# Mixed rows written to DRAM already transposed, block by block, by the vector engine

## The chip, the cores and the metric

The kernel runs on one core of one Trainium2 chip. The metric is the device time of one execution in microseconds (us). The engines named below are TensorE (PE; PEld is its weight load), VectorE (DVE), ScalarE (ACT), GpSimd (POOL) and SyncE (SP, which here only issues DMAs).

## The reference

Two layers of a token mixer over 2048 latent tokens and 256 context tokens, width 1024, in fp32. Cut to what matters here:

```python
h = layer_norm(x) * (1 + scale) + shift                  # and hc from the context
parts = split_cols(h @ w_in)                             # 15 groups of columns
hg  = bidirectional_recurrence(hgrn2_inputs(...))        # 256 wide, chunks of 64 tokens
gla = bidirectional_recurrence(gla_inputs(...))          # 256 wide
mla = softmax_attend(q, concat(k_c, k), concat(v_c, v))  # 4 heads, 512 wide, 2304 keys
y = concatenate([gated_head_norm(hg), mla * silu(mgate), gated_head_norm(gla)], -1)
x_new = layer_norm(ALPHA * x + gate * (y @ w_out)) * ln_g + ln_b
```

The last layer computes `x_new` for the latent tokens alone.

## The kernel before, in words

Tokens go in tiles of 128 (18 tiles, the first two are context) and in pairs of tiles (9 pairs). Each layer has three stages, and every intermediate goes through DRAM scratch (`scratch`, L111).

- `project` (L270): layer norm and the product with `w_in`, each fp32 operand split into a high and a low part, with three matmuls for a product.
- `mix` (L974): attention and the two recurrences, interleaved. Per tile, `attend` (L885) does two rounds of two heads: scores `pss`, exponentials `sx`, transposes of them `ptp`, split into `ph` (ACT) and `pl` (DVE), products `oc`, then `poa`, which DVE scales and gates into `ym` (L969). Per pair, `recur` (L668) works through six levels, POOL scaling keys `ka` and queries `qa` with decay products `t`; the level-0 product lies in a buffer of tag `t0` (L723). `chunk_outputs` (L796) takes the pair's output `o` (ACT, L821, into the one buffer of tag `acc`), squares it into a `t0` buffer (`sq`), reduces that on DVE (`rss`, L826 and L827), takes the power on POOL (`rrs`, L90) and multiplies twice on POOL (L830, L831).
- Both write rows of `y` (tokens by features) to DRAM: `recur` columns 0 to 511 of a pair at L832, `attend` columns 512 to 1023 of a tile at L972.
- `output` (L1040): per tile, `turned` (L1070) loads 128 rows of `y`, turns them with 8 TensorE transposes into `pty`, and splits them into `yhl` (ACT high, DVE low). 48 matmuls (two halves of 512 columns, 8 blocks of features, 3 products) go into `pzo`, and DVE forms `z` from them. `turned(t + 1)` stands ahead of the matmuls of tile t.

All engines run their instructions in order. The order on each engine is set when the kernel is built: a scheduler follows a simulated timeline, with priorities (`AHEAD`, `SOON`, `EARLY`). DMAs issued from SP go round eight completion counters (`DMAHW0` to `DMAHW7` in the order listings), and a DMA waits for the earlier one on its counter. Buffers of later stages lie on those of earlier ones, so the first writes of `output` wait for the last readers in `mix`.

Of the kernel before, what the change touches and what calls it, by code (L numbers as in the profile page):

```python
# [7 lines left out]
F32 = mybir.dt.float32  # L8
# [3 lines left out]
ALU = mybir.AluOpType  # L12
# [4 lines left out]
P = 128  # L17
D = 1024
KD = D // P
# [35 lines left out]
class Trunk:  # L55
# [55 lines left out]
    def scratch(self, l):  # L111

        d, c, nt = self.dpool, self.cpool, self.nt
        S = {}
# [11 lines left out]
        S["sb"] = d.tile([P, self.npairs, NCH, 3, 64], F32, name=f"dsb{l}")  # L126
        S["y"] = d.tile([nt, D], F32, name=f"dy{l}")
        return S
# [501 lines left out]
    def pair_rows(self, nat, p, c0, c1):  # L630
        return nat[p * SEG:(p + 1) * SEG, c0:c1].rearrange("(j p) n -> p j n", p=P)

    def back_states(self, S, rp, rps):

        nc = self.nc
# [4 lines left out]
        for p in list(range(ncp))[::-1] + list(range(ncp, self.npairs))[::-1]:  # L640
            f = rp.tile([P, 1 + L3], F32, tag="fa", name="bf")
            nc.gpsimd.memset(f[:, 0:1], 0.0)
            nc.sync.dma_start(out=f[:, 1:].rearrange("p (b n) -> p b n", b=3), in_=S["F"][:, p, 0])
            k = rp.tile([P, 3, SEG], F32, tag="ka", name="bk")
# [151 lines left out]
    def chunk_outputs(self, S, rp, rps, p, acc, qa, qm, v2, vt, sbt, sts):  # L796
        nc = self.nc
        po = rps.tile([P, 2, 512], F32, tag="R", name="po")
        quads = ((0, 0), (1, 1), (1, 0), (0, 1))
        for j in range(2):  # L800
            for sl in range(4):
                for e, c in quads:
                    rows = slice(64 * e, 64 * e + 64)
                    o = 256 * j + 64 * sl
# [26 lines left out]
        nc.gpsimd.tensor_tensor(o, o, vt[:, :, 512:1024], op=ALU.mult)  # L831
        nc.sync.dma_start(out=self.pair_rows(S["y"], p, 0, 512), in_=o)  # L832

# [51 lines left out]
    def attend(self, S, K, ap, aps, G, t, j):  # L885
        nc = self.nc
# [4 lines left out]
        nc.sync.dma_start(out=mg, in_=S["nat"][t * P:(t + 1) * P, 1024:1536])  # L891
        ym = ap.tile([P, 512], F32, tag="ym", name="ym")
        for hp in range(2):
# [70 lines left out]
            for i in range(2):  # L964
                nc.tensor.matmul(po[:, i, :], os_[:, i * P:(i + 1) * P], S["uv"][:, 2 * hp + i, :],  # L965
                                 start=True, stop=True)
            for i in range(2):
                hs = slice((2 * hp + i) * P, (2 * hp + i + 1) * P)
                nc.vector.scalar_tensor_tensor(out=ym[:, hs], in0=po[:, i, :], scalar=rinv[i], in1=mg[:, hs],  # L969
                                               op0=ALU.mult, op1=ALU.mult)  # L970
            yield
        nc.sync.dma_start(out=S["y"][t * P:(t + 1) * P, 512:1024], in_=ym)  # L972

    def mix(self, l, S):  # L974

        nc = self.nc
        with ExitStack() as ctx:
            rp = self.pool(ctx)
            ap = Route(lambda: self.pool(ctx), "os mx nm sm ri", "mg", "ym", "ph pl", "cth ctl ks", "cq cqh cql",
                       "qn ropt ropa ropb", "rh rl", "qh ql", "cnh cnl", "sx")  # L980
# [59 lines left out]
    def output(self, l, S):  # L1040
        nc, io = self.nc, self.io
        last = l == DEPTH - 1
        with ExitStack() as ctx:
            R = Route(lambda: self.pool(ctx), "yt", "woa", "sto mvo veo rso", "gate", "lng lnb", "z", "xto", "wob", "yhl")
            ps = Route(lambda: self.pool(ctx, psum=True), "low", "pz", "tr")
            nc.vector.memset(ps.tile([P, 512], F32, name="low")[:, 0:1], 0.0)
# [23 lines left out]
            def turned(t):  # L1070
                yt = R.tile([P, D], F32, tag="yt", bufs=2, name="yt")
                nc.sync.dma_start(out=yt, in_=S["y"][t * P:(t + 1) * P, :])
                yhl = R.tile([P, 2, KD, P], F32R, tag="yhl", bufs=2, name="yhl")
                yh, yl = yhl[:, 0], yhl[:, 1]
                for q in range(2):
                    pt = ps.tile([P, 4, P], F32, tag="tr", bufs=2, name="pty")
                    for i in range(4):
                        k = 4 * q + i
                        nc.tensor.transpose(pt[:, i, :], yt[:, k * P:(k + 1) * P], self.ident)  # L1079
                    self.split(yh[:, 4 * q:4 * q + 4, :], yl[:, 4 * q:4 * q + 4, :], pt)  # L1080
                return yh, yl
# [142 lines left out]
```

## Time and profile before

| | |
|---|---|
| median of 3 runs | 3767.64 us (3766.39 to 3768.89) |
| the profiled execution: its time | 3762.88 us |
| the profiled execution: its span | 3761.1 us |
| mean granted TensorE clock | 0.99 of full speed |
| PE busy | 3621.1 us (96%) |
| DVE busy | 2139.0 us (57%) |
| ACT busy | 1435.7 us (38%) |
| POOL busy | 812.2 us (22%) |
| DMA, queue of SP | 403 MB, 33.7% of 16 engines |

Busy time is the union of an engine's instructions over the span of the profiled execution. Matmuls overlap: a group's mean duration is longer than what one of them adds to the busy time. Layer 0's `mix` runs from about 640 to 1740 us, its `output` to about 1960; layer 1's `mix` from about 2580 to 3570, its `output` to the end.

### The profile page before, as it was taken

The page shows a single profiled execution, that of the slowest core. Times are in us where ns is not written, and L with a number is a line of the kernel's source. Part 1 is how long each engine was busy: PE and PEld are TensorE (multiplying, and loading weights), DVE is VectorE, ACT ScalarE, POOL GpSimd, SP SyncE. Part 2 cuts the span into 40 slices and gives each one's busy share as a digit, 9 for nine tenths or more (in the row PEclk, how much of TensorE's full clock was granted, in tenths as well). Part 3 has the DMA queues.
Part 4 walks back from the last instruction along what each step waited for, and adds up shares of the span by engine and source line. Part 5 has one row for each costly group of instructions (what it writes and reads, how often), then busy time and mean ns, then how long its engine had stood idle before and what let it go on. Part 6 is the DMA issues. An engine that isn't in the chain of part 4 may idle for free. (4 is left out here: it accounts for less than half of the span.)

```text
span 3761.1 us, 84541 instructions
## 1 busy us (share of the span) xinstructions
PE 3621.1 (96%) x36056; PEld 3274.7 (87%) x36056; DVE 2139.0 (57%) x5026; ACT 1435.7 (38%) x2296; POOL 812.2 (22%) x614
## 2 busy tenths in 40 slices
PE   8999999999999999998999999999999999999999
PEld 5999999888788888887879999998888888888787
DVE  6764242566666666556765442425765566656566
ACT  3525242344444444442115242523443444444400
POOL 1000000001335444351110000000022344644211
PEclk9999999999999999998999999999999999999999
DMA  7774344322122112115435443433221222221342
GB/s 255 232 202 147 124 135 140 111 80 91 53 65 84 61 56 70 54 58 196 156 106 163 146 147 120 153 109 110 85 88 43 60 68 61 71 80 44 102 143 101
DMA packets 263687, 410.79 MB, mean 109 GB/s; under 512 B 39632, under 2 KB 179984, under 8 KB 262288
## 3 DMA queue, kind: packets, MB, share of 16 engines
q1 hardware_dynamic: 261872, 403.04, 33.7%
q8 instruction: 283, 4.64, 0.5%
q10 hardware_dynamic: 1440, 2.36, 0.2%
q14 instruction: 92, 0.75, 0.1%
HBM read 288.66 MB, written 116.67 MB: 108 GB/s over the span
## 5 line engine op out<-in xcount | busy, mean ns | idle before, releaser
L420 PE MATMUL pj<-wh,hl 128*128 128x256 f32 (+1 forms) x2224 | 623.8, 281 | 8.0 <-DVE hl L85 8.0
L420 PE MATMUL pj<-wh,hh 128*128 128x256 f32 (+1 forms) x2224 | 625.2, 281 | 2.0 <-DVE ve L372 1.2
L420 PE MATMUL pj<-wl,hh 128*128 128x256 f32 (+1 forms) x2224 | 624.3, 281 | 0.0
L910 DVE TENSOR_SCALAR_CACHE_REDUCE sx<-pss 128x512 f32<-128x512 f32 (+1 forms) x648 | 402.9, 632 | 204.8 <-PE pss L908 178.7
L85 DVE TENSOR_TENSOR pl<-ptp,ph 128x512 fp32r<-128x512 f32 x580 | 389.1, 686 | 183.8 <-ACT ph L79 180.6
L79 ACT CAST ph<-ptp 128x512 fp32r<-128x512 f32 x580 | 327.9, 586 | 361.8 <-PE ptp L946 349.3
L420 PEld LDWEIGHTS pj<-wh,hl 128*128 128x128 f32 x2224 | 421.1, 190 | 8.9 <-DVE hl L85 8.9
L420 PEld LDWEIGHTS pj<-wh,hh 128*128 128x128 f32 x2224 | 423.2, 190 | 2.7 <-DVE ve L372 1.6
L420 PEld LDWEIGHTS pj<-wl,hh 128*128 128x128 f32 x2224 | 421.5, 190 | 0.0
L946 PE MATMUL ptp<-ident,sx 128*128 128x128 f32 x2320 | 372.0, 278 | 25.6 <-DVE pl L85 15.7
L933 PE MATMUL oc<-ph,cnh 128*128 128x256 f32 x1160 | 340.1, 315 | 23.4 <-ACT ph L79 22.9
L920 ACT ACTIVATE sx<-sx,nm 128x2304 f32<-128x2304 f32 (+1 forms) x136 | 288.4, 2121 | 183.0 <-DVE nm L916 182.6
L431 PE MATMUL pj<-hh,wh 128*128 128x256 f32 x1136 | 321.1, 283 | 0.0
L431 PE MATMUL pj<-hh,wl 128*128 128x256 f32 x1136 | 319.9, 282 | 0.0
L431 PE MATMUL pj<-hl,wh 128*128 128x256 f32 x1136 | 319.0, 281 | 0.0
L946 PEld LDWEIGHTS ptp<-ident,sx 128*128 128x128 f32 x2320 | 273.8, 142 | 50.5 <-DVE pl L85 19.8
L85 DVE TENSOR_TENSOR wl<-wraw,wh 128x1024 fp32r<-128x1024 f32 (+1 forms) x144 | 169.4, 1211 | 238.1 <-ACT wh L79 238.0
L933 PE MATMUL oc<-ph,cnl 128*128 128x256 f32 x1160 | 303.9, 284 | 0.0
L904 PE MATMUL pss<-cth,qh 128*128 128x512 f32 (+1 forms) x648 | 264.5, 408 | 13.3 <-DVE sx L910 13.3
L933 PEld LDWEIGHTS oc<-ph,cnh 128*128 128x128 f32 x1160 | 222.1, 191 | 52.1 <-ACT ph L79 39.0
L938 PE MATMUL oc<-pl,cnh 128*128 128x256 f32 x1160 | 245.2, 294 | 0.0
L905 PE MATMUL pss<-ctl,qh 128*128 128x512 f32 (+1 forms) x648 | 242.5, 374 | 0.0
(251 smaller groups left out, 7878.0 us busy)
## 6 DMA issues: line engine op xcount, KB each, us to landing
wraw<-in_w_in_dram SPq DMA_DIRECT2D x132, 512.0 KB, 4.6
dnat<-stg SPq DMA_DIRECT2D x104, 256.0 KB, 2.1
vg<-dnat SPq DMA_DIRECT2D x17, 1024.0 KB, 6.2
yt<-dy SPq DMA_DIRECT2D x34, 512.0 KB, 3.7
wmt<-in_w_modT_dram SPq DMA_DIRECT2D x64, 256.0 KB, 3.8
fa<-dF SPq DMA_DIRECT2D x18, 768.0 KB, 4.3
ka<-dK SPq DMA_DIRECT2D x18, 768.0 KB, 4.2
dK<-stg SPq DMA_DIRECT2D x36, 256.0 KB, 4.1
```

What stands on the lines that cost most here:

```text
L79: nc.scalar.copy(hi, src)
L85: nc.vector.tensor_tensor(lo, src, hi, op=ALU.subtract)
L420: nc.tensor.matmul(pj[:, j, :n], h[pr][a][:, k, tk], w[b][:, k, :n], start=(k == 0 and a + b == 0), stop=(k == KD - 1 and a == 1))
L431: nc.tensor.matmul(pj[:, j, :], w[b][:, k, cs], h[pr][a][:, k, :], start=(k == 0 and a + b == 0), stop=(k == KD - 1 and b == 1))
L904: nc.tensor.matmul(pss[:, :n], G["qh"][hp][:, i, tk], K["cth"][:, ks], start=True, stop=False)
L905: nc.tensor.matmul(pss[:, :n], G["qh"][hp][:, i, tk], K["ctl"][:, ks], start=False, stop=False)
L910: nc.vector.tensor_scalar(sx[:, ks], pss[:, :n], SCALE, None, op0=ALU.mult, op1=ALU.max, accum_out=mx[:, nb:nb + 1])
L920: nc.scalar.activation(sx[:, :nk], sx[:, :nk], AF.Exp, bias=nm, accum_out=sm)
L933: nc.tensor.matmul(oc, K[k][:, keys(kc, c)], ph[:, c, :], start=(kc + c == 0 and k == "cnh"), stop=False)
L938: nc.tensor.matmul(oc, K["cnh"][:, keys(kc, c)], pl[:, c, :], start=False, stop=(kc + c == nch - 1))
L946: nc.tensor.transpose(pt[:, c, i, :], pexp[i][:, (kc + c) * P:(kc + c + 1) * P], self.ident)
```

## The change

The scratch tensor `y` (tokens by features) becomes `yT` (features by tokens). Before the rows are stored, DVE transposes every block of 32 by 32 elements inside a tile; the move of whole blocks is left to the DMA, in `put_turned`: one DMA for each 32 partitions, which writes pieces of 32 tokens (128 bytes) to one feature each. The recurrences write `o` through a new tile `ot` (tag `t0`) in two calls of `put_turned` (8 DMAs of 512 pieces), the attention writes each round of two heads through `yo` (4 DMAs of 256 pieces). `turned` loads a tile of `yT` with one DMA of 512-byte rows and splits it without TensorE and without PSUM.

```diff
-        S["y"] = d.tile([nt, D], F32, name=f"dy{l}")
+        S["yT"] = d.tile([D, nt], F32, name=f"dy{l}")
...
+    def put_turned(self, S, src, f0, n, t0):
+
+        for a in range(4):
+            dst = S["yT"][f0:f0 + n, t0 + 32 * a:t0 + 32 * a + 32].rearrange("(b f) t -> f b t", f=32)
+            self.nc.sync.dma_start(out=dst, in_=src[32 * a:32 * a + 32].rearrange("f (b t) -> f b t", t=32))
...
         nc.gpsimd.tensor_tensor(o, o, vt[:, :, 512:1024], op=ALU.mult)
-        nc.sync.dma_start(out=self.pair_rows(S["y"], p, 0, 512), in_=o)
+        ot = rp.tile([P, 1024], F32, tag="t0", name="ot")
+        nc.vector.transpose(out=ot, in_=of)
+        for j in range(2):
+            self.put_turned(S, ot[:, 512 * j:512 * j + 512], 0, 512, (2 * p + j) * P)
...
-        ym = ap.tile([P, 512], F32, tag="ym", name="ym")
         for hp in range(2):
...
+            ym = ap.tile([P, 256], F32, tag="ym", name="ym")
             for i in range(2):
                 hs = slice((2 * hp + i) * P, (2 * hp + i + 1) * P)
-                nc.vector.scalar_tensor_tensor(out=ym[:, hs], in0=po[:, i, :], scalar=rinv[i], in1=mg[:, hs],
-                                               op0=ALU.mult, op1=ALU.mult)
+                nc.vector.scalar_tensor_tensor(out=ym[:, i * P:(i + 1) * P], in0=po[:, i, :], scalar=rinv[i],
+                                               in1=mg[:, hs], op0=ALU.mult, op1=ALU.mult)
+            yo = ap.tile([P, 256], F32, tag="yo", name="yo")
+            nc.vector.transpose(out=yo, in_=ym)
+            self.put_turned(S, yo, 512 + 256 * hp, 256, t * P)
             yield
-        nc.sync.dma_start(out=S["y"][t * P:(t + 1) * P, 512:1024], in_=ym)
...
-            ap = Route(lambda: self.pool(ctx), "os mx nm sm ri", "mg", "ym", "ph pl", "cth ctl ks", "cq cqh cql",
+            ap = Route(lambda: self.pool(ctx), "os mx nm sm ri", "mg", "ym yo", "ph pl", "cth ctl ks", "cq cqh cql",
...
-            ps = Route(lambda: self.pool(ctx, psum=True), "low", "pz", "tr")
+            ps = Route(lambda: self.pool(ctx, psum=True), "low", "pz")
...
-                yt = R.tile([P, D], F32, tag="yt", bufs=2, name="yt")
-                nc.sync.dma_start(out=yt, in_=S["y"][t * P:(t + 1) * P, :])
+                yt = R.tile([P, KD, P], F32, tag="yt", bufs=2, name="yt")
+                nc.sync.dma_start(out=yt, in_=S["yT"].rearrange("(k p) t -> p k t", p=P)[:, :, t * P:(t + 1) * P])
                 yhl = R.tile([P, 2, KD, P], F32R, tag="yhl", bufs=2, name="yhl")
                 yh, yl = yhl[:, 0], yhl[:, 1]
                 for q in range(2):
-                    pt = ps.tile([P, 4, P], F32, tag="tr", bufs=2, name="pty")
-                    for i in range(4):
-                        k = 4 * q + i
-                        nc.tensor.transpose(pt[:, i, :], yt[:, k * P:(k + 1) * P], self.ident)
-                    self.split(yh[:, 4 * q:4 * q + 4, :], yl[:, 4 * q:4 * q + 4, :], pt)
+                    ks = slice(4 * q, 4 * q + 4)
+                    self.split(yh[:, ks, :], yl[:, ks, :], yt[:, ks, :])
```

POOL at the turn from one pair of the recurrence to the next (layer 0, the fourth such turn), before. `rrs` and the two products into `o` belong to the old pair, the others to the new one; a number behind `t` only tells buffers apart.

```order
L764 TENSOR_TENSOR ka<-ka,fa 128x384
L724 TENSOR_TENSOR t_15606<-fa 128x768 [waits DVE_49]
L90 TENSOR_TENSOR rrs<-rss,mhalf 128x16 [waits DVE_49]
L764 TENSOR_TENSOR ka<-ka,t_15606 128x192x2x2 [waits Activation_49,Pool_49]
L724 TENSOR_TENSOR t_15647<-t_15606 128x384
L830 TENSOR_TENSOR o<-o,rrs 128x1024 [waits DMAHW0_49,Pool_49]
L724 TENSOR_TENSOR t_15688<-t_15647 128x192 [waits Pool_49]
L831 TENSOR_TENSOR o<-o,vg 128x1024 [waits DMAHW1_49,Pool_49]
```

The same place after the change:

```order
L770 TENSOR_TENSOR ka<-ka,fa 128x384
L90 TENSOR_TENSOR rrs<-rss,mhalf 128x16 [waits DVE_49]
L836 TENSOR_TENSOR o<-o,rrs 128x1024 [waits Activation_49,Pool_49]
L837 TENSOR_TENSOR o<-o,vg 128x1024 [waits Pool_49]
L770 TENSOR_TENSOR qa<-qa,fa 128x384 [waits PE_49]
L770 TENSOR_TENSOR qa<-qa,fa 128x384
L730 TENSOR_TENSOR t_15775<-fa 128x768 [waits DMAHW4_49,DMAHW3_49,DMAHW5_49,DMAHW2_49,DMAHW6_49,DMAHW1_49,DMAHW7_49,DMAHW0_49,DVE_49]
L770 TENSOR_TENSOR ka<-ka,t_15775 128x192x2x2 [waits Activation_49,Pool_49]
```

The old pair's three instructions now run together, and the level-0 product `t<-fa` has moved behind them; it waits for eight DMAs, the stores out of `ot`, because it shares the `t0` buffer.

DVE at the same turn after the change, from the last but one score piece ahead of `ot` to `yo`:

```order
L85 TENSOR_TENSOR pl<-ptp,ph 128x512 [waits Activation_49]
L918 TENSOR_SCALAR sx,mx<-pss 128x512 [waits PE_49]
L839 STREAM_TRANSPOSE ot<-o 128x1024 [waits Pool_49]
L918 TENSOR_SCALAR sx,mx<-pss 128x512 [waits PE_49]
L918 TENSOR_SCALAR sx,mx<-pss 128x256 [waits PE_49]
L978 SCALAR_TENSOR_TENSOR ym<-poa,ri,mg 128x128 [waits PE_49]
L978 SCALAR_TENSOR_TENSOR ym<-poa,ri,mg 128x128
L923 TENSOR_REDUCE nm<-mx 128x1 [waits DVE_49]
L981 STREAM_TRANSPOSE yo<-ym 128x256 [waits DMAHW2_49,DMAHW1_49,DMAHW3_49,DMAHW0_49,DVE_49]
```

Without `ot` and `yo` the listing of before reads the same here. Seven instructions on `pl` and `sx` stand between `rss` (L833) and `ot`, and `ot` waits for POOL.

DVE where layer 1's `output` begins, before, from the attention's last product:

```order
L969 SCALAR_TENSOR_TENSOR ym<-poa,ri,mg 128x128 [waits PE_49]
L969 SCALAR_TENSOR_TENSOR ym<-poa,ri,mg 128x128
L1046 MEMSET low 128x1 [waits DVE_49]
L1102 TENSOR_TENSOR z<-pzo,gate 128x512 [waits DMAHW7_49]
L1102 TENSOR_TENSOR z<-pzo,gate 128x512 [waits PE_49]
```

And after:

```order
L978 SCALAR_TENSOR_TENSOR ym<-poa,ri,mg 128x128 [waits PE_49]
L978 SCALAR_TENSOR_TENSOR ym<-poa,ri,mg 128x128
L981 STREAM_TRANSPOSE yo<-ym 128x256 [waits DMAHW6_49,DMAHW5_49,DMAHW7_49,DMAHW0_49,DVE_49]
L1057 MEMSET low 128x1
L85 TENSOR_TENSOR yhl<-yt,yhl 128x512 [waits DMAHW5_49,Activation_49]
L85 TENSOR_TENSOR yhl<-yt,yhl 128x512 [waits Activation_49]
L1110 TENSOR_TENSOR z<-pzo,gate 128x512 [waits DMAHW5_49,DMAHW4_49,DMAHW6_49,DMAHW3_49,DVE_49]
L1110 TENSOR_TENSOR z<-pzo,gate 128x512
```

The first `z` waited for the one store of the last `ym`; it now waits for the four stores of the last `yo`.

## Rows read from the trace of the kernel before

**Rows 1.** The page's first part: busy us, share of the span, instructions.
```profile
PE 3621.1 (96%) x36056; PEld 3274.7 (87%) x36056; DVE 2139.0 (57%) x5026; ACT 1435.7 (38%) x2296; POOL 812.2 (22%) x614
```
**Rows 2.** Stretch: us, PE, PEld, DVE, ACT, POOL busy, PE clock, DMA share, GB/s.
```profile
640.00:1700.00 1060.00, 1012.38 (x12484) 894.35 (x12483) 650.63 (x1703) 461.93 (x726) 362.41 (x256) 1.00 0.23 72
2580.00:3545.00 965.00, 930.66 (x11198) 809.89 (x11198) 610.82 (x1623) 433.34 (x663) 333.39 (x240) 0.99 0.23 71
3600.00:3700.00 100.00, 100.00 (x466) 81.78 (x465) 67.23 (x102) 8.61 (x16) 13.11 (x9) 1.00 0.38 134
```
**Rows 3.** Instructions by line: all transposes into `pty`.
```profile
L1079 PE MATMUL pty<-ident,yt 128*128 128x128 f32 x272 | 36.4, 273 | 1.1 <-DVE yhl L85 1.0
```
**Rows 4.** Timeline of PE over one steady tile (start us, us, what).
```profile
3608.70 1.03 PE L1079 MATMUL pty<-ident,yt 128*128 128x128 f32 x8
...
3610.28 0.40 PE L1099 MATMUL pzo<-wo,yhl 128*128 128x512 f32 x1
3610.98 0.40 PE L1099 MATMUL pzo<-wo,yhl 128*128 128x512 f32 x1
...
3620.73 1.04 PE L1079 MATMUL pty<-ident,yt 128*128 128x128 f32 x8
```
**Rows 5.** Instructions by line: the low half of the split in `output`.
```profile
L85 DVE TENSOR_TENSOR yhl<-pty,yhl 128x512 fp32r<-128x512 f32 x68 | 45.9, 680 | 5.0 <-ACT yhl L79 4.9
```
**Rows 6.** Timeline of DVE and PE where layer 1's `output` begins.
```profile
3569.66 0.61 DVE L969 SCALAR_TENSOR_TENSOR ym<-poa,ri,mg 128x128 f32<-128x128 f32 x2 [5.67 <-PE poa L965]
3572.62 1.29 DVE L1102 TENSOR_TENSOR z<-pzo,gate 128x512 f32<-128x512 f32 x2 [2.22 <-DMA dy<-ym]
```
**Rows 7.** Timeline of PE where layer 0's `output` begins.
```profile
1747.13 0.80 PE L1099 MATMUL pzo<-wo,yhl 128*128 128x512 f32 x1 [5.77 <-DVE z L1102]
1752.36 0.40 PE L1099 MATMUL pzo<-wo,yhl 128*128 128x512 f32 x1
```
**Rows 8.** Issue on SP of a load with exchanged dimensions (ns: min/median/max).
```profile
L692 SPq DMA_DIRECT2D v<-dnat x34: 579/614/1852, 705.1 to 3435.9; - x34
```
**Rows 9.** DMA issues by line: KB each, median us to landing.
```profile
ropt<-in_rope_dram SPq DMA_DIRECT2D x16, 128.0 KB, 2.7
ropt<-in_rope_dram SPq DMA_DIRECT2D x32, 64.0 KB, 2.2
gate<-mc SPq DMA_DIRECT2D x2, 4.0 KB, 12.1
```
**Rows 10.** Instructions by line: DVE work nearest to the new transposes.
```profile
L81 DVE CAST hh<-hf 128x1024 fp32r<-128x1024 f32 x32 | 21.3, 688 | 22.1 <-PE pj L420 16.3 <-ACT hf L389 5.7
L826 DVE TENSOR_REDUCE rss<-sq 128x16 f32<-128x1024 f32 x17 | 20.7, 1219 | 50.9 <-ACT sq L824 50.9
```
**Rows 11.** Who waited for whom: us in total, times, longest us.
```profile
POOL qa L764 <- PE pa L788: 373.4, 102, 18.0
ACT acc L790 <- DMA dy<-o: 14.9, 12, 2.0
```
**Rows 12.** Timeline of POOL at one turn of pairs, layer 0.
```profile
1118.02 2.30 POOL L764 TENSOR_TENSOR ka<-ka,fa 128x384 f32<-128x384 f32 x2
...
1121.70 2.90 POOL L90 TENSOR_TENSOR rrs<-rss,mhalf 128x16 f32<-128x16 f32 x1
...
1127.54 1.91 POOL L830 TENSOR_TENSOR o<-o,rrs 128x1024 f32<-128x1024 f32 x1
...
1129.87 2.42 POOL L831 TENSOR_TENSOR o<-o,vg 128x1024 f32<-128x1024 f32 x1
1132.25 1.00 POOL L724 TENSOR_TENSOR t<-t 128x96 f32<-128x96 f32 x3
1141.79 2.35 POOL L764 TENSOR_TENSOR qa<-qa,fa 128x384 f32<-128x384 f32 x2 [8.54 <-PE pa L788]
```
**Rows 13.** Timeline of DVE at the same turn.
```profile
1117.21 0.76 DVE L827 TENSOR_SCALAR rss<-rss 128x16 f32<-128x16 f32 x1
...
1126.63 0.69 DVE L910 TENSOR_SCALAR_CACHE_REDUCE sx<-pss 128x512 f32<-128x512 f32 x1 [1.01 <-PE pss L908]
```

## The prediction

> **What bounds the kernel now.** First the busy shares [rows 1]: PE works 96% of the span, the next engine, DVE, 57%. So time is won where PE's work or PE's waits get shorter, and lost where something makes PE wait. Second, the stages [rows 2]: steady `output` has no idle PE at all (100.00 of 100 us), while the two `mix` stretches have 47.6 and 34.3 us of idle PE, 82 us together, with DVE busy 61% and 63% of the time. Third, what the change takes off PE: the 272 transposes into `pty` cover 36.4 us of PE's busy time [rows 3], or 1.07 us a tile over 34 tiles. That is the most they can cost, because the first matmul behind them overlaps their end. Fourth, one steady tile [rows 4]: from one set of transposes to the next it takes 12.03 us, and three matmuls take 0.70, so 48 take 11.20 and the 8 transposes really cost 0.83 us.
>
> **What `output` wins.** In the order of before, 48 of the 272 transposes stand ahead of the last `poa` of their layer, among attention work that itself waits; the other 224 belong to 28 steady tiles. These win 28 x 0.83 = 23.2 us. The other 6 tiles' transposes partly fill waits: between 0 and 6 x 0.83 = 5.0, and I take half, 2.5. Together 25.7 us (ends 23.2 and 36.4). The split of a tile stays the same instructions of the same shape; only the source moves from PSUM to SBUF, and I keep 680 ns for its DVE half [rows 5]. In the steady stretch DVE is busy 67.2 of 100 us [rows 2], or 8.1 us a tile, so a tile of 11.20 us still hides all of it; if that cover went, DVE would bind at 8.1, which is below 11.20. The load of a tile now comes in pieces of 512 B instead of rows of 4 KB; it is issued two tiles ahead, and the DMA engines are 38% busy there [rows 2], so I cost it at nothing; were it late, PE would wait for all that exceeds some 20 us.
>
> **What the start of `output` loses.** The first `z` waits until the stores of the attention's last result have landed. In layer 1 before, `ym` is ready at 3570.27 and `z` starts at 3572.62, 2.35 us later, with DVE idle [rows 6]; PE had matmuls enough to cover it. After, `yo` comes first (0.35 us, below), then four issues instead of one. The nearest row for an issue with exchanged dimensions is 614 ns [rows 8], so 4 x 0.6 = 2.4 us, then a landing of 2.2 us for 64 KB in small pieces [rows 9], then 0.65 for `z`: with the 0.61 of `ym` [rows 6], 6.2 us from the end of `poa`. The new order on PE leaves 5 matmuls on `pzo` between the last `poa` and the point where both `pz` buffers are full, 1.2 us. So PE waits some 5 us in layer 1. In layer 0 PE already waits 5.77 us at this place [rows 7], and there 22 matmuls (5.1 us) stand behind `poa` to cover the longer chain; I cost it at nothing. A wait has a second price: after the 5.77 us, 12 matmuls take 5.23 us instead of 12 x 0.233 = 2.80 [rows 4, 7], 2.4 us lost at the lower granted clock. Sum for layer 1: 5 + 2.4, or 7 us (ends 0 and 12, the latter with a landing twice as long as 2.2 in both layers).
>
> **The stores.** 17 pairs give 8 DMAs each and 68 rounds give 4 each: 408 issues in place of 51. At 0.6 us they are 4.8 us a pair and 2.4 us a round, on a queue that mostly waits. Per piece of 128 B: the step from 64 to 128 KB in pieces of 256 B is 0.5 us for 256 pieces, 16 on each of 16 engines, at most 31 ns each [rows 9]; this is the row nearest in size, and half the bytes should cost no more. A pair's 4096 pieces are 256 an engine, at most 8 us; below I set no end, since the issues then set the pace. The far end is the store of 4-byte pieces, 12.1 us until it lands for two times 64 pieces an engine, 95 ns each, of which the trace does not show how much was waiting behind loads [rows 9]. I take 20 ns, 5 us a pair, which the issues hide. The Trainium skill (DMA: Bandwidth & Descriptors, Specifications) names 512 B as the smallest transfer at line rate and says that below it the engine reads, modifies and writes. That speaks against this change, and is the third rival below; the 256-byte loads of rows 9 do not show it, since they read DRAM.
>
> **DVE.** `ot` is 128 by 1024: between the 688 ns of a cast and the 1219 ns of a reduction of that shape [rows 10]. I take 1.2, since a transposition is no plain copy. `yo` is 128 by 256: between a quarter of 688 and half of 1219; I take 0.35. Together 17 x 1.2 + 68 x 0.35 = 44 us of DVE work in stretches where it has 61% to 63%. PE's waits there, for all causes, are 82 us beside 1261 us of DVE work [rows 2], 6.5%, so 44 us would bring about 3 us. On top of that `ot` blocks DVE while POOL finishes. At the turn shown, POOL is free of `ka<-ka,fa` at 1120.32 and `rss` is ready at 1117.97; with `rrs` and both products behind each other, 2.90 + 1.91 + 2.42 = 7.2 us, `o` is ready at 1127.6 [rows 12, 13]. DVE ends the seventh instruction behind `rss` at about 1127.3 [rows 13]. So DVE stands for some 0.3 us and then is busy for 1.2; behind it queue a `sx` for which PE holds two buffers. I put 0.2 us of PE on each of 17: 3 us. DVE together 6 us (ends 0, and 17 x 1.5 + 68 x 0.35 = 49).
>
> **POOL.** The new wait is `t<-fa`, which needs the 8 stores out of `ot`. From `o` at 1127.6: 0.3 + 1.2 for `ot`, 8 x 0.6 of issues, 2.2 of landing give 1136.1. Queued behind it are `t<-fa` and the next decay products and keys, which before POOL had done by 1133.25, ahead of an idle stretch of 8.54 us [rows 12]: 12.9 us without a gap from 1120.32, less the 7.2, are 5.7 us. After, POOL is done with them at 1141.8, against 1141.79 for the next `qa<-qa,fa`, which PE releases. So the cover is just enough, and I cost it at nothing; for 102 such waits POOL has 373.4 us, 3.7 each, in reserve [rows 11]. `acc` becomes free when `ot` is read, not when a store lands: ACT's 14.9 us of waiting go [rows 11]. Little of it reached PE; I take 2 us (ends 0 and 14.9).
>
> **Sum.** 3762.9 (the profiled execution's time, 1.8 above its span) - 25.7 + 7 + 6 - 2 = 3748.2. The median of the runs is 4.8 above the profiled one, so 3753.
>
> **Rivals.** (1) The whole gain: PE sheds all 36.4 us, nothing waits: 3767.6 - 36.4 = 3731. For it speaks that PE is the bound everywhere and that DVE and POOL have reserves; against it, the 48 transposes that fill waits, and the new wait of the first `z`. (2) The gain is eaten in `mix`: DVE's 49 us reach PE to a half or more, 3753 - 6 + 25 = 3772, at most 3796. It decides against the change from 20 us of PE on. For it speaks that `ot` waits for POOL in the middle of the attention; against, that 17 reductions of the same length [rows 10] stand there already, beside only 82 us of idle PE in all. (3) Slower: small stores are dear. At 95 ns a piece a pair's stores take 24 us, not 4.8 + 2.2; `t<-fa` comes some 17 us later, two levels' reserve (7.4) covers part, and PE waits some 10 us at each of 15 turns: 3753 + 150 = 3903. It decides from about 37 ns a piece on, where the stores take longer than their issues by the reserve of one level and 1 us more, which 15 turns make into the gain. By the Trainium skill's rule on 512 B this is the likely side; the trace has no store of this size.
>
> **How the numbers follow.** A kernel here tells from no change what exceeds 0.2%, 7.5 us. Chances: forecast 0.50 (3742 to 3764), whole gain 0.16, eaten in `mix` 0.24 (3762 to 3796), dear stores 0.10. Faster than 3760.1: 0.16 + 0.44 = 0.60. Within 0.2%: 0.06 + 0.17 = 0.23. Slower: 0.07 + 0.10 = 0.17. The range reaches from 3734, which leaves out a part of the whole gain, to 3778, which leaves out the dear stores and the end of the second rival. The likeliest case's own range is 3742 to 3764.
>
> **What would show it.** Steady `output`: the spacing of tiles 11.2 us, PE without idle time, and no `pty`. Layer 1's start: PE waits about 5 us for the first `z`, behind the stores of `yo`, and the clock falls after it. `mix`: `STREAM_TRANSPOSE` of 1.2 and 0.35 us; idle PE near 90 us, not 82; the packets of the stores near 20 ns; POOL's wait for `t<-fa` a few us. The prediction is wrong if that last wait passes 10 us a turn, if SP's issues take much over 0.6 us each, or if the tiles of `output` come at a pace that PE doesn't set.

## The result, and the profile after

The changed kernel takes 3794.61 us (median of 3 runs, 3789.21 to 3795.09), 1.0069 times the kernel before (95% interval 1.0055 to 1.0083): slower, and outside the predicted range of 3734 to 3778. The profiled execution has a time of 3795.09 and a span of 3793.3 us.

First the stages: starts of the last product of the attention (`poa`) in each layer and of the last matmul of layer 0's `output` (view by line, one window for each stage; behind the colon ns min/median/max, then the first and the last start). Before:

```profile
L965 PE MATMUL poa<-uv,os x144: 270/275/377, 748.7 to 1738.6; 128*128 128x128 f32 x144
L965 PE MATMUL poa<-uv,os x128: 270/275/377, 2621.6 to 3569.3; 128*128 128x128 f32 x128
L1101 PE MATMUL pzo<-wo,yhl x288: 389/395/632, 1722.4 to 1954.8; 128*128 128x512 f32 x144
```

After:

```profile
L973 PE MATMUL poa<-uv,os x144: 270/275/582, 749.6 to 1766.3; 128*128 128x128 f32 x144
L973 PE MATMUL poa<-uv,os x128: 270/275/377, 2642.4 to 3609.1; 128*128 128x128 f32 x128
L1109 PE MATMUL pzo<-wo,yhl x288: 389/395/628, 1760.8 to 1974.6; 128*128 128x512 f32 x144
```

Up to layer 0's last `poa` the kernel lost 27.7 us, from there to the last `pzo` it won 7.9, up to layer 1's last `poa` it lost 20.0, and to the end it won 7.6. So `mix` lost 47.7 and `output` won 15.5: 32.2 together, the difference of the two spans. The experiments' table uses these two sums. (`mix` includes `project` here, which moved by 1 us a layer. And what PE does of `output` ahead of a last `poa` counts to `mix`: in the trace 83 matmuls on `pzo` before and 69 after, so 14 of them, 3.3 us at 0.233, moved into `output`.)

Busy shares, from the page:

```profile
PE 3624.1 (96%) x35784; PEld 3262.6 (86%) x35784; DVE 2167.9 (57%) x5111; ACT 1438.6 (38%) x2296; POOL 810.8 (21%) x614
```

The same two stretches of `mix` as in [rows 2], with the same columns, and 100 us of steady `output`:

```profile
640.00:1700.00 1060.00, 1004.72 (x12270) 880.55 (x12273) 645.12 (x1699) 443.52 (x701) 349.17 (x251) 0.98 0.25 69
2580.00:3545.00 965.00, 924.59 (x11131) 801.43 (x11130) 605.56 (x1617) 418.72 (x645) 319.87 (x237) 0.99 0.25 69
3640.00:3740.00 100.00, 100.00 (x432) 80.78 (x431) 71.73 (x108) 10.19 (x18) 12.82 (x9) 1.00 0.43 142
```

PE has 272 instructions fewer than in [rows 1] and yet is no less busy. In `mix` its idle time is 55.3 + 40.4 = 95.7 us (82 before), and it got through fewer matmuls in the same stretch. Who waited for whom (us in total, times, longest):

```profile
ACT km L760 <- POOL ka L770: 79.8, 30, 5.5
POOL t L730 <- DMA dy<-yo: 51.5, 7, 11.0
PEld pa L794 <- POOL qa L770: 30.1, 23, 4.2
PE pa L794 <- POOL qa L770: 20.9, 14, 3.8
POOL t L730 <- DMA dy<-ot: 14.6, 4, 8.9
POOL t L730 <- DVE sx L918: 10.4, 1, 10.4
POOL t L730 <- DVE pl L85: 9.8, 1, 9.8
ACT acc L796 <- DVE ot L839: 14.0, 11, 3.7
POOL qa L770 <- PE pa L794: 297.2, 72, 18.0
```

Before:

```profile
ACT km L754 <- POOL ka L764: 3.9, 2, 3.3
PE pa L788 <- POOL qa L764: 1.5, 4, 0.8
```

So the keys and queries now come late. POOL's level-0 product waits 66.1 us for stores in 11 turns. (A wait for many semaphores is put down to the last: `t<-fa` waits for those of `ot`, which share their counters with `yo`.) Two more waits, 20.2 us, are put down to DVE, but there too the last store out of `ot` was issued only 2.5 and 2.8 us before the product began: 86.3 us in 13 turns. One turn in detail, the one of [rows 12]; POOL:

```profile
1130.07 2.30 POOL L770 TENSOR_TENSOR ka<-ka,fa 128x384 f32<-128x384 f32 x2
1132.33 2.91 POOL L90 TENSOR_TENSOR rrs<-rss,mhalf 128x16 f32<-128x16 f32 x1
1135.31 1.90 POOL L836 TENSOR_TENSOR o<-o,rrs 128x1024 f32<-128x1024 f32 x1
1137.30 2.40 POOL L837 TENSOR_TENSOR o<-o,vg 128x1024 f32<-128x1024 f32 x1
1149.41 1.47 POOL L730 TENSOR_TENSOR t<-fa 128x768 f32<-128x768 f32 x1 [9.71 <-DMA dy<-yo]
1150.83 2.33 POOL L770 TENSOR_TENSOR qa<-qa,fa 128x384 f32<-128x384 f32 x2
1153.12 2.19 POOL L770 TENSOR_TENSOR ka<-ka,t 128x768 f32<-128x768 f32 x1
```

SP's issues, DVE, and PE's scores of levels 0, 1 and 2, same turn:

```profile
1141.01 6.28 SPq L637 DMA_DIRECT2D dy<-ot  x8
1147.38 1.93 SPq L637 DMA_DIRECT2D dy<-yo  x4
...
1139.73 1.25 DVE L839 STREAM_TRANSPOSE ot<-o 128x1024 f32<-128x1024 f32 x1 [0.37 <-POOL o L837]
...
1144.12 2.36 PE L794 MATMUL pa<-qa,km 64*64 64x64 f32 x64
1153.34 1.82 PE L794 MATMUL pa<-qa,km 64*64 64x64 f32 x64
1160.94 1.32 PE L794 MATMUL pa<-qa,km 64*64 64x64 f32 x32 [2.14 <-POOL qa L770]
```

The same scores before:

```profile
1139.32 2.35 PE L788 MATMUL pa<-qa,km 64*64 64x64 f32 x64
1144.82 1.82 PE L788 MATMUL pa<-qa,km 64*64 64x64 f32 x64
1149.13 1.08 PE L788 MATMUL pa<-qa,km 64*64 64x64 f32 x29
```

From `o` to the product: 1.3 us for `ot`, 6.3 for eight issues, 2.1 of landing, 9.7 together. Level 0 to level 2 takes 16.8 us, 9.8 before. The scores are a chain: POOL's queries and keys, ACT's copy `km`, PE, POOL again. What starts late stays late. And PE's wait of 2.14 us has a price behind it. The 3.4 us from 1161.82 on (windows, columns as in [rows 2]):

```profile
1161.82:1165.20 3.38, 3.38 (x51) 3.15 (x48) 1.33 (x1) 0.93 (x2) 3.20 (x4) 0.50 0.02 5
```

PE is busy throughout, at a granted clock of 0.50 (1.2 GHz of 2.4). Over the 1060 us of layer 0's `mix` shown above the clock is 0.98, 1.00 before.

Not all turns are like this one. Of the 15 turns at which a new pair follows, 8 have this order, the product ahead of `qa<-qa,fa`, and POOL stands idle for 8.8 to 11.0 us in each of them. In the other 7 the queries come first, as in the listing in "The change", and the product then waits 2.3 us at most. The turn of that listing:

```profile
1315.41 2.34 POOL L770 TENSOR_TENSOR qa<-qa,fa 128x384 f32<-128x384 f32 x2 [7.52 <-PE pa L794]
1317.71 1.47 POOL L730 TENSOR_TENSOR t<-fa 128x768 f32<-128x768 f32 x1
```

The new operations, and the split of a tile, by line:

```profile
L85 DVE TENSOR_TENSOR yhl<-yt,yhl 128x512 fp32r<-128x512 f32 x68 | 46.2, 687 | 3.0 <-ACT yhl L79 2.9
L981 DVE STREAM_TRANSPOSE yo<-ym 128x256 f32<-128x256 f32 x68 | 30.2, 444 | 1.0
L839 DVE STREAM_TRANSPOSE ot<-o 128x1024 f32<-128x1024 f32 x17 | 21.1, 1243 | 10.2 <-POOL o L837 10.2
```

Loads and stores of `yT` by DMA (KB each, median us to landing):

```profile
yt<-dy SPq DMA_DIRECT2D x34, 512.0 KB, 4.7
dy<-yo SPq DMA_DIRECT2D x272, 32.0 KB, 1.7
dy<-ot SPq DMA_DIRECT2D x136, 64.0 KB, 3.6
```

Steady `output`: DVE's timeline, the second `z` of a tile and of the next:

```profile
3651.06 0.69 DVE L1110 TENSOR_TENSOR z<-pzo,gate 128x512 f32<-128x512 f32 x1 [2.60 <-PE pzo L1109]
...
3662.22 0.69 DVE L1110 TENSOR_TENSOR z<-pzo,gate 128x512 f32<-128x512 f32 x1 [2.60 <-PE pzo L1109]
```

The start of layer 0's `output`: PE's first matmul behind the wait (timeline), and the 3.41 us behind it with their neighbours (windows, columns as in [rows 2]):

```profile
1778.82 0.80 PE L1107 MATMUL pzo<-wo,yhl 128*128 128x512 f32 x1 [7.18 <-DVE z L1110]
```

```profile
1779.41:1782.82 3.41, 3.41 (x9) 2.64 (x8) 3.34 (x7) 0.00 (x0) 0.56 (x1) 0.50 0.51 140
1783.14:1790.00 6.86, 6.86 (x31) 5.56 (x30) 3.60 (x5) 0.00 (x0) 0.65 (x1) 1.00 0.38 136
1758.00:1778.80 20.80, 13.09 (x60) 10.40 (x60) 10.78 (x17) 7.28 (x11) 0.00 (x0) 0.94 0.94 305
```

A tile takes 11.16 us in place of 12.03 [rows 4]: what was promised for steady `output` came. At the start of layer 0's `output`, after 7.18 us of idle time, the granted clock is 0.50 (1.2 GHz) for 3.41 us, in which eight matmuls start every 0.43 us instead of 0.23; before, 12 matmuls ran so [rows 7]. And ahead of it the DMA engines are 94% busy with loads, those of `output` and of layer 1's weights, behind which SP issues the stores of the last `yo` and among which they have to land.

### The profile page after: what moved, and what is told of

The parts are those of the page before. It is cut to its first block, busy times and chain, and to the rows that moved or that the text cites. A ratio compares the mean times of both kernels' runs of the same rounds, so it can differ in the third digit from the quotient of the medians.

```text
span 3793.3 us, 84659 instructions
## 1 busy us (share of the span) xinstructions
PE 3624.1 (96%) x35784; PEld 3262.6 (86%) x35784; DVE 2167.9 (57%) x5111; ACT 1438.6 (38%) x2296; POOL 810.8 (21%) x614
## 5 line engine op out<-in xcount | busy, mean ns | idle before, releaser
L794 PEld LDWEIGHTS pa<-qa,km 64*64 64x64 f32 (+1 forms) x6528 | 187.0, 137 | 72.2 <-POOL qa L770 30.1
```

Of the source, the lines that this page charges most:

```text
L794: nc.tensor.matmul(out, w, mv, start=True, stop=True, tile_position=pos)
```

## The experiments

Theory: the loss is the t0 buffer, **held** by the stores out of `ot`, so that POOL's level-0 product comes late. Rivals: the transposes as **DVE work** (51 us more), and the **issues** or pieces of 408 small stores. All runs, with ratios to the kernel before on the same chip; the last two columns are changes of one profiled execution against that of before, so their sum can miss the median's change by up to 12 us (most in e5 and e11, whose profiled execution was the slowest of its runs).

| run | median us | ratio (95%) | mix | output |
|---|---|---|---|---|
| changed kernel | 3794.6 | 1.0069 (1.0055–1.0083) | +47.7 | -15.5 |
| e1 swap | 3775.4 | 1.0030 (1.0018–1.0041) | +32.0 | -16.9 |
| e2 attention half | 3771.2 | 1.0017 (1.0008–1.0025) | +8.0 | +0.7 |
| e3 recurrence half | 3798.4 | 1.0091 (1.0078–1.0105) | +46.3 | -12.2 |
| e4 hold alone | 3794.3 | 1.0081 (1.0068–1.0095) | +25.5 | +4.6 |
| e5 ot in vg | 3766.0 | 1.0002 (0.9993–1.0011) | +22.1 | -11.1 |
| e6 e5, ym at the top | 3806.7 | 1.0106 (1.0091–1.0120) | +64.5 | -27.1 |
| e7 DVE work alone | 3789.3 | 1.0065 (1.0051–1.0079) | +16.6 | +7.4 |
| e8 stores alone | 3762.9 | 0.9992 (0.9984–1.0001) | -6.9 | +6.5 |
| e9 before, scores whole | 3747.3 | 0.9942 (0.9929–0.9954) | -16.9 | -0.7 |
| e10 hold, scores whole | 3773.3 | 1.0018 (1.0009–1.0026) | +9.8 | -0.1 |
| e11 changed, scores whole | 3785.7 | 1.0048 (1.0035–1.0061) | +48.4 | -16.8 |
| e12 e5, scores whole | 3742.8 | 0.9929 (0.9916–0.9942) | -7.3 | -11.2 |
| e13 e7, scores whole | 3778.3 | 1.0033 (1.0021–1.0045) | +7.7 | +7.3 |
| e14 e12, ym moved | 3720.6 | 0.9880 (0.9863–0.9896) | -14.8 | -21.7 |
| e15 e1, scores whole | 3764.4 | 1.0000 (0.9991–1.0010) | +14.6 | -17.5 |
| e16 e5, ym moved | 3749.9 | 0.9949 (0.9937–0.9962) | +12.1 | -20.8 |
| e17 e9, ym moved | 3745.2 | 0.9938 (0.9926–0.9951) | -9.8 | -9.9 |
| e18 o's transposes, whole | 3752.5 | 0.9957 (0.9944–0.9971) | -15.5 | +1.6 |

**e1.** Two buffers exchanged.

```diff
-        o = rp.tile([P, 2, 512], F32, tag="acc", name="o")
+        o = rp.tile([P, 2, 512], F32, tag="t0", name="o")
-        sq = rp.tile([P, 1024], F32, tag="t0", name="sq")
+        sq = rp.tile([P, 1024], F32, tag="acc", name="sq")
-        ot = rp.tile([P, 1024], F32, tag="t0", name="ot")
+        ot = rp.tile([P, 1024], F32, tag="acc", name="ot")
```

> The changed kernel with two buffers exchanged: o lies in the buffer of tag t0, its square and the transposed ot in that of tag acc. All DVE transposes and all 408 small stores stay; POOL's level-0 product t<-fa then waits for DVE's transpose alone, no longer for the eight stores out of ot, and the next wait for those stores is ACT's copy into acc, as it was before the change. Theory 'held buffer' (POOL's product waits for the stores, 66 us in all, so queries and keys come late to TensorE): mix gives back most of the 47 us that it lost, the time falls to 3745 to 3765 us, and POOL's waits for DMA at the product are gone. Rival 'DVE work' (51 us of transposes delay sx, pl and ym): no change, 3785 to 3800. Rival 'many issues' (408 issues of 0.4 to 0.5 us on SP make loads late): no change either, 3785 to 3800.

POOL waits for no store any more, and 19 us come back, less than expected. ACT's copy into `acc` now waits 29.5 us for the stores, so e1 also adds a wait.

**e2 and e3.** One half turned on DVE, the other stored by rows and turned by TensorE: the put_turned call and the transpose of one half go, and `output` keeps four of its eight transposes.

> Only the attention's half of the rows is turned on DVE and stored feature by feature (68 transposes of 444 ns, 272 small stores); the recurrences store o by rows as before, and output turns their four blocks of features on TensorE. Held buffer: this half holds no t0, so mix loses almost nothing; output gains half of its gain, about 12 us less the start of about 4: 3755 to 3765 us. DVE work: 30 of the 51 us of transposes are here, so mix loses about 28 us of the 47: 3780 to 3790. Many issues: two thirds of the issues are here, so mix loses about 31 us: 3783 to 3793.

> Only the recurrences' half is turned on DVE (17 transposes of 1243 ns through the t0 buffer, 136 small stores); the attention stores ym by rows as before. Held buffer: the whole wait of POOL is here, mix loses about 40 of the 47 us and output gains about 10: 3790 to 3800 us. DVE work: 21 of 51 us are here, mix loses about 19 us: 3773 to 3783. Many issues: one third, mix loses about 16: 3770 to 3780.

Nearly the whole loss lies in the recurrences' half, with a third of the stores and 21 of 51 us of DVE work; two thirds of the stores cost `mix` 8 us. Shares by DVE time or by issues are refuted. e2 is 6 us above the range expected for held buffers: half the transposes less gave `output` nothing, since its wait for the first `z` rose to 15.4 us.

**e4.** The kernel before with the hold alone.

```diff
-        nc.gpsimd.tensor_tensor(o, o, vt[:, :, 512:1024], op=ALU.mult)
-        nc.sync.dma_start(out=self.pair_rows(S["y"], p, 0, 512), in_=o)
+        ot = rp.tile([P, 2, 512], F32, tag="t0", name="ot")
+        nc.gpsimd.tensor_tensor(ot, o, vt[:, :, 512:1024], op=ALU.mult)
+        nc.sync.dma_start(out=self.pair_rows(S["y"], p, 0, 512), in_=ot)
```

> The kernel before with one thing of the change alone: POOL's second product writes its result into the t0 buffer, and the one store of rows goes out from there. No DVE transpose, no small store, no change in output. The level-0 product of the next pair then waits for that one store (512 KB). Held buffer: the store takes some 3 to 5 us from issue to landing, less than the eight stores, so mix loses something, 10 to 30 us: 3778 to 3798. DVE work and many issues: same as before, 3764 to 3772.

The hold alone costs 29 us by the medians, with one store a pair and no transposes. Its waits:

```profile
ACT km L754 <- POOL ka L764: 54.2, 23, 5.7
POOL t L724 <- DMA dy<-ot: 45.0, 13, 3.8
```

PE's idle time grew little here; its busy time rose by 25.5 us, 18 of them in the scores `pa` (249.7 to 267.9 us for the same 7616 matmuls; counted from each start to the next, without idle time, 14). In TensorE's order those stand in 278 pieces, 217 before: the scheduler had put more other work between them. That was a new theory, for e9 to e12.

**e5 and e6.** `ot` in the used-up half of `vg`; in e6 the buffers of `ym` and `yo` also moved to the end of mix's pools.

```diff
-        ot = rp.tile([P, 1024], F32, tag="t0", name="ot")
-        nc.vector.transpose(out=ot, in_=of)
         for j in range(2):
-            self.put_turned(S, ot[:, 512 * j:512 * j + 512], 0, 512, (2 * p + j) * P)
+            nc.vector.transpose(out=vt[:, j, 512:1024], in_=o[:, j])
+            self.put_turned(S, vt[:, j, 512:1024], 0, 512, (2 * p + j) * P)
```

> The changed kernel with the transposed o written into the upper half of vg (the gate that POOL's second product has just used up), by two transposes of 128x512. So t0 is held by nothing new, and acc is free as soon as DVE has read o; what waits for the stores is only the next pair's load of vg, which is needed late in a pair. All DVE work and all 408 stores stay. Held buffers (t0 in the changed kernel, t0 shortly and acc for longer in the run with exchanged buffers): mix loses less than 10 us, and the output's gain of some 15 us stands: 3752 to 3764 us. DVE work, or many issues: as with exchanged buffers, 3770 to 3780.

> The run with ot in vg, and in it the buffers of ym and yo moved to the end of mix's pools, where no buffer of output lies on them. The first z of each output stage then waits for no store of yo. First z (TensorE waits 12.2 us for z in the two output stages of the changed kernel, 5.8 before, and its clock falls after it): 6 to 12 us less than the run without the move. If that wait only shifts to the next thing that output needs (the load of the last rows): no difference, within 3 us.

e5: 29 us come back with t0 free, to 2 us above the range expected; in the profiled execution `mix` still loses. e6: the wait for the first `z` fell as expected, from 15.9 to 3.0 us, but the move shifted all other buffers, and at the start of `mix` PE waits 39.0 us for `cqh`, a wait that was not there:

```profile
L862 PE MATMUL pq<-cqh,mh 128*128 128x256 f32 x136 | 42.4, 312 | 39.2 <-ACT cqh L79 39.0 <-DVE ql L85 0.2
```

**e7 and e8.** The kernel before with DVE's work alone, and with the small stores alone.

```diff
+        for j in range(2):
+            nc.vector.transpose(out=vt[:, j, 512:1024], in_=o[:, j])
...
+            nc.vector.transpose(out=mg[:, 256 * hp:256 * hp + 256], in_=ym[:, 256 * hp:256 * hp + 256])
```

> The kernel before with the DVE transposes alone: o is transposed into the used-up half of vg and each half of ym into the used-up half of mg, and nobody reads either. Stores, output and the t0 buffer are those of before. It is about 51 us more of DVE work, with the in-order waits of DVE for POOL's o. Held buffers: within 5 us of before, 3762 to 3771. DVE work: this is the whole loss of mix that the held buffer doesn't explain, 15 to 30 us more than before: 3780 to 3796.

> The kernel before with the small stores alone: o and the halves of ym go out untransposed in the same 408 DMAs of 128-byte pieces, each tile's pieces anywhere in its own 128 rows of y, so that the numbers in y are permuted and the output isn't the reference's. No DVE transpose, t0 as before, output as before. Many issues, or dear pieces: 15 us or more above before, 3780 to 3800. Held buffers and DVE work: within 6 us of before, 3760 to 3772, with ACT's wait at acc (14.9 us) a little longer since o goes out in eight DMAs.

In e8 the numbers of `y` lie in permuted places, and `ym` has two buffers of half the size. The stores cost nothing: refuted as a cause, with one limit. The 32 pieces of a row lie side by side in e8, while in the changed kernel each piece goes to another row, 9216 bytes on; that these cost nothing is not shown by e8 (a piece takes 13 ns in the median there, 12 in e8, and e14, below, has all of them). The transposes alone cost 23 us, as the DVE rival had it.

**e9 to e12.** The same priority on the score matmuls in four kernels; 119 pieces in each.

```diff
-                    nc.tensor.matmul(out, w, mv, start=True, stop=True, tile_position=pos)
+                    with self.tc.high_priority(offset=1000):
+                        nc.tensor.matmul(out, w, mv, start=True, stop=True, tile_position=pos)
```

> The kernel before, with a higher scheduling priority (1000) on the score matmuls of the recurrence (pa), so that in TensorE's order the 64 matmuls of one level stand together: 119 pieces in place of 217. Nothing else is edited. It is the base for the three runs beside it. Theory 'cut scores' (a level's 64 small matmuls cost more TensorE time each time that other matmuls are put between them; pa is busy 249.7 us in 217 pieces, 267.9 in the 278 of the run with the hold alone): pa's busy time falls by 20 to 50 us, and the time may fall by as much, 3720 to 3760. Rival: the pieces cost nothing, and whole levels make TensorE wait for POOL's keys at the head of its queue: 3768 to 3800.

> The run with the hold alone (t0 held by one store of rows), with the same priority on pa: 119 pieces in place of 278. Cut scores: the hold cost 29 us mostly because the scheduler, seeing the level-0 product late, cut the scores into 61 more pieces; with equal pieces it stands at most 10 us above the run beside it. If the wait itself costs (POOL 45 us behind the store, and TensorE behind POOL): still 25 us or more above it.

> The changed kernel with the same priority on pa: 119 pieces in place of 247. Cut scores: of its 27 us above before some 16 were pa's busy time; it stands within 12 us of the run of the kernel before with whole scores. If the waits themselves cost: 25 us or more above it.

> The run with ot in vg, with the same priority on pa: 119 pieces in place of 235. Cut scores: pa loses its 9 us over the kernel before, so it stands 5 to 15 us below the kernel before with whole scores. If DVE's in-order work costs by itself: no lower than it.

Cut scores do cost (e9, 18 us less, `pa` 225.2 us), but they don't explain the hold: with equal pieces it still costs 26 us (e10 against e9), and the changed kernel 43 more than with t0 free (e11 against e12). e12 itself is 4.5 us below e9, just short of what was expected and within the noise. Who waits, e9:

```profile
ACT km L754 <- POOL ka L764: 19.1, 7, 3.9
```

and e10:

```profile
ACT km L754 <- POOL ka L764: 78.9, 31, 6.0
POOL t L724 <- DMA dy<-ot: 52.8, 15, 4.9
```

So the late product costs either way: as idle time where scores stand whole, as cut scores where the scheduler fills the time.

**e13 to e15.** The transposes alone (e7), e12 with another place for `ym` and `yo`, and the exchanged buffers (e1), all with whole scores. The edit of e14:

```diff
-"mg", "ym yo", "ph pl", "cth ctl ks",
+"mg", "ph pl", "ym yo", "cth ctl ks",
```

> The kernel before with the DVE transposes alone (into used-up halves of vg and mg, read by nobody) and with whole scores: 119 pieces of pa. The kernel before with whole scores took 3747 us. If the 23 us that these transposes cost without the priority are DVE's work in DVE's order: 3765 to 3772. If they were the cut scores and the luck of an order: within 8 us of 3747, 3740 to 3755.

> The run with ot in vg and whole scores (3743 us), with the buffers of ym and yo moved behind those of ph and pl, so that they lie under output's second xto and no longer under its first z. In the run without the move TensorE waited 16.2 us for z at the two starts of output, and the clock fell after it. First z: that wait falls to about 3 us, the time by 8 to 16: 3727 to 3735. If the wait moves on to the next load or the start of mix gets worse: 3740 or more.

> The run with exchanged buffers (o in t0, square and ot in acc), with whole scores. POOL's level-0 product of the next pair waits for DVE's transpose and for no store; ACT's copy into acc waits for the stores. With t0 held by the stores the changed kernel with whole scores took 3786 us, with t0 free it took 3743. If the stores make the hold dear: 3745 to 3757. If any hold of t0 past POOL's two products does: 3765 to 3780.

e13 came out above both of its ranges, e14 6 us below the one expected. e14 is the fastest kernel of this study, 1.2% below before. `pzo` (busy us, mean ns, idle before it) in e12:

```profile
L1107 PE MATMUL pzo<-wo,yhl 128*128 128x512 f32 x544 | 218.2, 401 | 17.4 <-DVE z L1110 16.2 <-ACT yhl L79 1.1
```

and in e14:

```profile
L1107 PE MATMUL pzo<-wo,yhl 128*128 128x512 f32 x544 | 216.7, 398 | 4.4 <-DVE z L1110 3.8 <-ACT yhl L79 0.4
```

The wait fell by 12.4 us, the time by 22; the rest is partly clock (mean granted 0.95 in both starts of `output` in e12, 0.98 and 1.00 in e14). Of the 7 us that stand in `mix`, 5 are work of `output`: 74 matmuls on `pzo` run ahead of the last `poa` in e12, 52 in e14. e15 lies between t0 free (e12) and t0 held by stores (e11), 22 us over e12, and in neither of its ranges, just below the one for any hold. POOL waits 20.4 us for DVE's `ot` there, but ACT's copy into `acc` also waits 37.4 us for stores; the two prices are not separated.

**e16 to e18.** e16 is e14 without the priority; e17 the kernel before with the priority and `ym` moved; e18 is e13 without the transposes of `ym`.

> The changed kernel with its two buffer repairs and no priority: ot in the used-up half of vg, and the buffers of ym and yo behind those of ph and pl. Held buffers: the run with ot in vg alone took 3766 us; without the wait for the first z it falls by 10 to 20, to 3746 to 3757, below the kernel before. If an order of its own decides more than these waits: anywhere from 3760 to 3780.

> The kernel before with the two edits that are not the change: whole scores, and the buffer of ym behind those of ph and pl, so that its first z waits for no store either (TensorE waited 4.5 us for it in the run with whole scores, 3747 us). If the change itself is worth its removed transposes: 3739 to 3747, so that the run with all repairs of the changed kernel (3721) stands 18 to 26 below it. If the 22 us that the move gave there were luck of an order that the kernel before has as well: 3720 to 3732.

> The kernel before with whole scores and the DVE transposes of o alone (34 of 689 ns into the used-up half of vg, read by nobody); those of ym are left out. If the transpose of o, behind POOL's products in DVE's order, makes the 31 us: 3768 to 3780. If the 68 transposes of ym do, which stand between DVE's work on scores: within 8 us of 3747. By DVE time, 23 of 53 us, it would be 3760.

With its two buffers repaired the change is faster than before by 0.5%. Against a kernel before that has the same other edits, it is worth 0.9880 / 0.9938 = 0.9942, 22 us (14 to 30 by the two intervals): near the 25.7 that were predicted for `output`. In e13's 31 us, the transposes of `o` have 5, within the noise, and those of `ym` 26.

## Why the prediction was wrong, step by step

- **What `output` wins: right.** 11.16 us a tile, predicted 11.20; no `pty`; DVE's half of the split 687 ns, predicted 680. e14 against e17 comes near the sum.
- **The start of `output`: right for layer 1, 1.4 us off in layer 0.** PE's wait for `z` is 12.2 us in both layers, 7.2 of it in layer 0, so 5.0 in layer 1, as predicted. In layer 0 the 22 matmuls did not cover all of the longer chain: the wait was 5.8 before. `yo` was ready at 1767.66 and SP, busy with loads, issued its stores from 1770.16 to 1772.82; they landed among those loads, and `z` began at 1778.07. The clock fell there as it had before. `output` won 15.5 of the 18.7 us that these steps left it, and the 14 matmuls that moved into it make up the other 3.
- **The stores: right.** 442 and 505 ns median an issue (0.6 predicted), 1.7 us to landing for 32 KB; e8 prices the stores at nothing; a piece took 13 ns median in the trace's DMA packets (20 predicted). So the third rival's mechanism is refuted. By the Trainium skill (DMA: Bandwidth & Descriptors, Specifications) pieces under 512 B are read, modified and written; no cost of that shows in e8. What did show is SP: at the turn above eight issues took 6.28 us, not 4.8.
- **POOL: the step that failed.** "So the cover is just enough, and I cost it at nothing." The chain was well sized: from the end of `ka<-ka,fa` to `t<-fa` 15.8 us predicted (1120.3 to 1136.1), 17.0 measured (1132.37 to 1149.41). The cover was not: 8.54 us of idle POOL [rows 12] ended when PE's level-0 scores were done, and that moment was taken from the old order. In it these scores began 19.0 us after `ka<-ka,fa`; in the new one 11.8 (1144.12). `qa<-qa,fa` could have run at 1146.5 and ran at 1150.83, behind the waiting product; the keys of level 1, ready at 1126.8 before, came at 1155.3. The reserve of "373.4 us, 3.7 each" [rows 11] covered a part only: POOL's waits for these scores fell to 297.2 us, 76 less against 86 of new waiting, and yet the queries and keys came late to PE and ACT, since what delays a chain also delays the point at which such a wait ends. The prediction's sum has 8.5 us of waiting in it (1127.6 to 1136.1), its list of signs "a few us"; its sign of being wrong, more than 10 us, showed in three turns. Price: 26 to 43 us in three pairs of runs (e4 with before, e10 with e9, e11 with e12), 29 in the fourth (changed kernel and e5).
- **The clock in `mix`: left out.** The prediction gave waits their "second price" at the start of `output` alone. The three executions of the changed kernel have a mean granted clock of 0.985 to 0.986, those of the kernel before beside the experiments 0.987 to 0.991, 0.989 in the median. An estimate from these: 0.004 of 3794 us, at most 15 of the 27 us lost, are matmuls at the lower clock behind waits. It is no other name for the hold: e10 and e9 have the same clock (0.986), and so nearly have e4 and the kernel before (0.9885, 0.989), while e11 (0.982) against e12 (0.986) may have 15 of its 43 us from it.
- **DVE: its size is unsettled.** `ot` 1243 and `yo` 444 ns (1.2 and 0.35 predicted). Their price was put at 6 us, ends 0 and 49; alone they cost 23 (e7) and 31 (e13), 26 of these by the transposes of `ym`. A part of that is not in `mix`: 7.4 us of e7's stand in `output`, where PE waits 12.1 us for the first `z` (5.8 before), and 7.3 of e13's (12.7 us, 4.5 in e9). Another part is clock: 0.984 in the median of e13's executions, 0.989 in e18's, at most 19 of the 26 us by the same estimate. Yet e14 runs all of them, and against e17 gets nearly the whole gain. Work in DVE's order can't be the price by itself; which order or wait makes it was not found.
- **ACT's waits for `acc`: wrong.** Not 14.9 us gone, but 14.0 for `ot` in place of the store.

## What to carry to other kernels

A buffer that is shared across a turn of a loop is a wait: before a long-lived tile (here one that stores read) goes into a scratch buffer, ask which engine writes that buffer next, and put the tile where the next writer is a load that is needed late. Idle time of an engine inside a dependency chain is a poor reserve: when the order changes, the point where it ends moves too, so cover must be counted in the new order. A short wait of PE can cost more than itself, when the granted clock falls behind it. Where a change wins in one stage and loses in another, price the halves and each side effect alone: here the same change is 0.7% slower with one buffer tag and 0.5% faster with two others.

## What the runs showed of the hardware

- Stores of 128-byte pieces to DRAM, side by side in a row, cost no time here: 408 DMAs of them in place of 51 gave 0.9992 (0.9984 to 1.0001), and 64 KB landed in 2.0 us median in e8. To scattered rows 64 KB landed in 3.6 us out of `ot`, eight stores in a row, and in 1.9 out of `vg` in e5, four and four; why these differ is not shown.
- In `mix` too the granted clock falls behind a wait: after PE's 2.14 us at the turn above it is 0.50 for 3.4 us of full work.
- DVE transposes 32 by 32 blocks of fp32 in 444 ns for 128x256, 689 for 128x512 and 1243 for 128x1024.
- The 64-row score matmuls cost TensorE more when other matmuls stand between them: the same 7616 are busy 225.2 us in 119 pieces (e9) and 267.9 in 278 (e4). A part of this is overlap with the neighbours; from each start to the next it is 217.1 and 248.7 us.
